# Layer norm lines in halves of 512 columns, and low weight parts formed row block by row block, in a two-layer hybrid trunk

## The chip, the cores and the metric

The kernel runs on one core of a Trainium2 chip. The time is device microseconds (us) of one execution, from launch to end; three executions of the kernel before gave a median of 1139.65 us. One more execution was recorded by the hardware profiler, and everything said about where the time goes comes from that one. TensorE (PE) multiplies matrices, VectorE (DVE) and ScalarE (ACT) work on rows of data, GpSimd (POOL) does the same more slowly, SyncE (SP) issues transfers. PEld is the loading of PE's stationary operand, which overlaps PE.

## The reference, cut to what matters

512 tokens of width 1024 go through two layers. Each has a token mixer and a dense MLP with 4096 hidden columns, and after each of these four sub-layers comes a residual sum and a layer norm.

```python
def layer_norm(x, g, b):
    xf = x.astype(jnp.float32)
    mu = jnp.mean(xf, axis=-1, keepdims=True)
    var = jnp.mean(jnp.square(xf - mu), axis=-1, keepdims=True)
    return ((xf - mu) * lax.rsqrt(var + LN_EPS) * g + b).astype(x.dtype)

def squared_relu_mlp(x, w_up, w_down):
    return jnp.square(jax.nn.relu(x @ w_up)) @ w_down

h = x
for i in range(DEPTH):                     # DEPTH = 2
    mix = dsa_mixer(h, ...) if i % 2 == 0 else gla_mixer(h, ...)
    h = layer_norm(DN_ALPHA * h + mix, ln_mix_g[i], ln_mix_b[i])
    h = layer_norm(DN_ALPHA * h + squared_relu_mlp(h, mlp_w_up[i], mlp_w_down[i]), ln_mlp_g[i], ln_mlp_b[i])
```

The first mixer is sparse attention: an indexer scores all causal keys, each query keeps the best 128 and attends to these alone. The second is gated linear attention (GLA) in chunks. All data and weights are float32.

## The kernel before, in words

**Matrix products.** Each float32 operand is split into a high part (fp32r) and a low part, the remainder. A product is three matmuls: high times high, high times low, low times high (`mm3`, lines 198, 199 and 200). Weights arrive by DMA in units of 256 rows by up to 512 columns, as a tile `raw` of two row blocks of 128 (line 133). `split` makes of such a unit `w_hi` on ACT (line 142) and `w_lo` on DVE (line 143), one operation each for both row blocks. A panel is 4 such units for most products and 7 for a step of the MLP's down product, which uses a recursive scheme with sums of weight blocks formed on POOL (`t`, lines 164 to 172). Panels are requested one ahead of use, and six buffers of each of `w_hi` and `w_lo` exist, so a unit is split when PE is done with an earlier one.

**A layer norm** takes one tile of 128 tokens by 1024 columns. Per token tile: the last matmul result is added in (`accumulate`, line 291, which also sums the row), ACT squares and sums (line 303), DVE forms the variance (lines 317 to 320, `ve` being the last), ACT takes the root (line 269), DVE refines the reciprocal (lines 270 to 273). Two long lines on DVE do the rest: line 325, `y = (y - mean) * g`, and line 326, `y = y * r + b`. Before, each is one operation of 1024 columns, except in the last layer norm, where each is two of 512, since the result goes out by halves.

**The handoff.** After a layer norm the tile is turned for the next product: `to_xt` lets PE do eight 128x128 transposes in two groups of four, one group for each half of the columns (line 247, tile `tps`); ACT copies each group to the high part of `XT` (line 250) and DVE forms the low part (line 251). PE's program goes on with other matmuls between a tile's last product and its transposes.

**Order.** Each engine runs its instructions in one fixed order, which a scheduler chooses when the program is built, from priorities (`urgent` raises them) and its own estimates of durations. An instruction waits on semaphores for others; all behind it on the same engine wait with it. So the place of the transposes among the matmuls in PE's order says when the scheduler thought the layer norm would be ready.

**Stages** by the time at which they run in the profile: sparse attention with its projections to about 222 us, its layer norm to 256, the first MLP to 560, its layer norm, overlapped with the first GLA products, to 592, GLA to 785, its layer norm to 810, the second MLP to 1115, the last layer norm and the output to the end. The GLA stage has small masked products: `prepare` builds the tiles `Q` and `E` on POOL, ACT and DVE, `apply` multiplies them on PE into `qk` (lines 1025 and 1034) and DVE takes the result over into `near` (lines 1039 and 1048).

Of the kernel before, what the change touches and what calls it, by code (L numbers as in the profile page):

```python
# [14 lines left out]
F32 = mybir.dt.float32  # L15
# [11 lines left out]
DM = 1024  # L27
# [79 lines left out]
class Trunk:  # L107
    def __init__(self, tc, es):
        self.tc, self.nc = tc, tc.nc
        self.const = es.enter_context(tc.tile_pool(name="const", bufs=1))  # L110
        self.small = es.enter_context(tc.tile_pool(name="small", bufs=4))
        self.xt_p = es.enter_context(tc.tile_pool(name="xt", bufs=1))
        self.XT = self.xt_p.tile([P, 2, KT, SEQ], F32R, name="XT")
        self.raw_p = es.enter_context(tc.tile_pool(name="raw", bufs=RAW_BUFS))
        self.w_p = es.enter_context(tc.tile_pool(name="w", bufs=W_BUFS))
        self.mm = es.enter_context(tc.tile_pool(name="mm", bufs=3, space=PSUM))
        self.qk = es.enter_context(tc.tile_pool(name="qk", bufs=2, space=PSUM))
        self.po = es.enter_context(tc.tile_pool(name="po", bufs=1, space=PSUM))
        self.tp = es.enter_context(tc.tile_pool(name="tp", bufs=2, space=PSUM))
        self.big = es.enter_context(tc.tile_pool(name="big", bufs=4))  # L120
        self.sums = [self.const.tile([P, 2], F32, name=f"sums{t}") for t in range(NT)]
        self.panels = []
        self.pending, self.turns, self.depth = [], 0, 1
        self.loaded = []
        self.taken = 0


    def fetch(self, w, r0, cols):
# [8 lines left out]
    def split(self, src):  # L137

        n = src.shape[2]
        hi = self.w_p.tile([P, 2, 512], F32R, name="w_hi")[:, :, :n]  # L140
        lo = self.w_p.tile([P, 2, 512], F32R, name="w_lo")[:, :, :n]
        self.nc.scalar.copy(hi, src)  # L142
        self.nc.vector.tensor_sub(lo, src, hi.bitcast(F32))  # L143
        return hi, lo

    def _load(self, i):
# [160 lines left out]
    def layer_norm(self, y, s, st, g, b, out=None):  # L307

        nc = self.nc
        d = self.small.tile([P, 1], F32, name="d")
        e = self.small.tile([P, 1], F32, name="e")
        nmu = self.small.tile([P, 1], F32, name="nmu")
        ve = self.small.tile([P, 1], F32, name="ve")
        nc.vector.tensor_sub(d, s[:, 0:1], s[:, 1:2])
        nc.vector.tensor_scalar(nmu, s[:, 0:1], s[:, 1:2], -1.0 / DM, op0=OP.add, op1=OP.mult)
        nc.vector.scalar_tensor_tensor(e, d, -1.0 / DM, d, op0=OP.mult, op1=OP.mult)
        nc.vector.tensor_scalar(ve, e, st["q"][:, 0:1], st["q"][:, 1:2], op0=OP.add, op1=OP.add)  # L320
        r = self.rsqrt(ve, 1.0 / DM)
        step = DM if out is None else DM // 2
        for c in range(0, DM, step):
            cs = slice(c, c + step)
            nc.vector.scalar_tensor_tensor(y[:, cs], y[:, cs], nmu, g[:, cs], op0=OP.add, op1=OP.mult)
            nc.vector.scalar_tensor_tensor(y[:, cs], y[:, cs], r, b[:, cs], op0=OP.mult, op1=OP.add)
            if out is not None:
                nc.sync.dma_start(out[:, cs], y[:, cs])
# [301 lines left out]
    def attention(self, x, xs):  # L630

        nc, tc = self.nc, self.tc
        with tc.tile_pool(name="att", bufs=1) as ap:
# [70 lines left out]
            def top_k():  # L704

                for b in range(1, NT):
                    for i in range(TOP_K // 8):
                        m8 = self.small.tile([P, 8], F32, name="m8")
                        nc.vector.max(out=m8, in_=sc[b])  # L709
                        nc.vector.match_replace(out=sc[b], in_to_replace=m8, in_values=sc[b], imm_value=NEG_TAKEN)  # L710
                        if i == TOP_K // 8 - 1:
                            nc.vector.tensor_scalar(sc[b], sc[b], NEG_SPLIT, -BIG, op0=OP.is_ge, op1=OP.mult)
                        if i % 4 == 3:
                            yield
# [107 lines left out]
            def blocks():  # L822

                for j in range(4):
                    logits(0, j)
                turned = []
                for i, (b, g) in enumerate(steps):
                    if (b, g) == (STACKED, 0):
                        split_v()
                    for x in range(4):  # L830
                        if i + 1 < len(steps):
                            logits(i + 1, x)
                        if x <= b:
                            turn(i, x)
                            if b >= STACKED:
                                turned.append((i, x))
                        if len(turned) > LAG:
                            values_t(*turned.pop(0))
                    if i > 0 and steps[i - 1][0] < STACKED:
                        values(i - 1)  # L840
                    yield
                for a in turned:
                    values_t(*a)
                for f in live.pop("back"):
                    f()

            with tc.tile_pool(name="rt", bufs=2) as self.rt, tc.tile_pool(name="p", bufs=2) as pp, \
                    tc.tile_pool(name="pT", bufs=8) as ptp, tc.tile_pool(name="on", bufs=1) as op_:
                self.rt_h = 8
                tk, bl = top_k(), blocks()  # L850
                for _ in range(4):
                    next(tk)
                u = self.next_panel()
                for t in range(NT):
                    ps = self.natural(u, t, 0, 512)
                    self.stack_q(self.rotated(ps, t, 8), 8, qT[t][:, 0:8, :])
                    next(tk)
                at = [0]

                def item():  # L860
                    next(bl)
                    if 3 <= at[0] < 7:
                        next(tk)
                    at[0] += 1

                u = self.next_panel()
                for t in range(NT):
                    ps = self.natural(u, t, 0, 512)
                    self.stack_q(self.rotated(ps, t, 8), 8, qT[t][:, 8:16, :])
                    if t % 2:  # L870
                        for _ in range(A_KV):
                            item()
                self.flush()
                wu = self.next_panel()
                for _ in range(A_KV):
                    item()
                self.load_residual(x)
                for t in range(NT - 1):
                    item()
                    self.out_first(wu, t)  # L880
                for _ in bl:
                    pass
                self.out_first(wu, NT - 1)
# [394 lines left out]
```

## Time and profile before

| what | value |
|---|---|
| median of three executions | 1139.65 us (1139.53 to 1140.13) |
| the profiled execution's own time | 1141.91 us |
| its span, first to last instruction | 1140.1 us |
| mean granted clock of TensorE | 0.991 |
| DVE busy | 888.6 us in 1592 instructions |
| ACT busy | 564.0 us |
| POOL busy | 213.7 us |

The span is 1.8 us shorter than the same execution's time, and that execution took 2.26 us longer than the median. Matmuls overlap their neighbours, so a PE that is busy need not be at its peak: the distance from one matmul's start to the next tells its pace. Idle time of an engine counts only where another one ends up waiting for it. In rows of the timeline the first two numbers are start and duration in us; a row marked x2 merges two instructions; what stands in brackets is the idle time ahead of it on its engine and what ended it.

### The profile page before, as it was taken

How to read it: one execution, taken by the hardware profiler on the slowest of the kernel's cores; microseconds unless marked ns; L12 is line 12 of the kernel's file. 1: busy time of each engine (PE TensorE's matmuls, PEld its weight loads, DVE VectorE, ACT ScalarE, POOL GpSimd, SP SyncE). 2: the span in 40 equal slices, each digit the busy share in tenths (PEclk: the TensorE clock that was granted, in tenths of full speed). 3: DMA queues.
4: the chain of work that ended last, by engine and by line, in shares of the span. 5: the costliest groups of instructions: out<-in, count | busy, mean ns of one | idle time of the engine just before them, and what ended most of it. 6: DMA issues, size and time to landing. Idle time of an engine off the chain costs nothing.

```text
span 1140.1 us, 16063 instructions
## 1 busy us (share of the span) xinstructions
PE 1124.3 (99%) x6040; PEld 948.2 (83%) x6040; DVE 888.6 (78%) x1592; ACT 564.0 (49%) x974; POOL 213.7 (19%) x136
## 2 busy tenths in 40 slices
PE   8999999999999999999999999999999999999997
PEld 7888988889888888888897897888988888888885
DVE  7899897697966976786985488667696976786787
ACT  6755686644533444444355476435353444444342
POOL 0000000002132123213300266110042123213221
PEclk9999899999999999999999999999999999999998
DMA  7222120521422422431522223152222422431421
GB/s 252 99 74 75 37 90 23 154 76 51 145 63 87 148 87 62 148 113 51 146 76 86 87 78 107 40 148 74 81 87 93 148 82 67 148 112 51 134 74 74
DMA packets 58198, 109.12 MB, mean 96 GB/s; under 512 B 5205, under 2 KB 10841, under 8 KB 58121
## 3 DMA queue, kind: packets, MB, share of 16 engines
q1 hardware_dynamic: 56968, 103.91, 29.0%
q0 software_dynamic: 1152, 4.19, 1.3%
q8 instruction: 47, 0.77, 0.3%
q14 instruction: 31, 0.25, 0.1%
HBM read 105.99 MB, written 2.10 MB: 95 GB/s over the span
## 4 chain that ended last, share of the span: by engine, by line
PE 87%; DVE 10%; issue 2%; ACT 1%; POOL 0%; DVEq 0%; ACTq 0%
PE ps L198 22%; PE ps L199 21%; PE ps L200 21%; DVE w_lo L143 2%; PE tps L247 2%; PE po L198 2%; PE po L199 2%; PE po L200 2%; PE tps L745 2%; DVE sc L710 1%; DVE m L709 1%; PE qk L200 1%; PE tps L198 1%; PE qk L198 1%; PE tps L200 1%
## 5 line engine op out<-in xcount | busy, mean ns | idle before, releaser
L143 DVE TENSOR_TENSOR w_lo<-raw,w_hi 128x1024 fp32r<-128x1024 f32 (+4 forms) x220 | 290.9, 1341 | 28.2 <-ACT w_hi L142 25.8
L142 ACT CAST w_hi<-raw 128x1024 fp32r<-128x1024 f32 (+4 forms) x220 | 223.1, 1024 | 115.6 <-PE ps L200 41.0
L198 PE MATMUL ps<-XT,w_hi 128*128 128x512 f32 (+2 forms) x648 | 237.3, 367 | 0.0
L199 PE MATMUL ps<-XT,w_hi 128*128 128x512 f32 (+2 forms) x648 | 237.2, 366 | 0.0
L200 PE MATMUL ps<-XT,w_lo 128*128 128x512 f32 (+2 forms) x648 | 237.0, 366 | 0.0
L198 PE MATMUL ps<-w_hi,XT 128*128 128x512 f32 (+4 forms) x432 | 161.9, 375 | 1.3 <-ACT w_hi L142 1.3
L199 PE MATMUL ps<-w_lo,XT 128*128 128x512 f32 (+4 forms) x432 | 158.6, 367 | 0.5 <-DVE w_lo L143 0.5
L200 PE MATMUL ps<-w_hi,XT 128*128 128x512 f32 (+4 forms) x432 | 158.6, 368 | 0.0
L198 PEld LDWEIGHTS ps<-XT,w_hi 128*128 128x128 f32 (+1 forms) x648 | 121.7, 188 | 20.3 <-issue 0.2
L199 PEld LDWEIGHTS ps<-XT,w_hi 128*128 128x128 f32 (+1 forms) x648 | 121.7, 188 | 20.2 <-issue 0.4
L200 PEld LDWEIGHTS ps<-XT,w_lo 128*128 128x128 f32 (+1 forms) x648 | 121.7, 188 | 20.2 <-issue 0.2
L164 POOL TENSOR_TENSOR raw<-raw 128x1024 f32<-128x1024 f32 x14 | 34.1, 2438 | 386.3 <-DVE w_lo L143 386.3
L200 PE MATMUL ps<-w_hi,form 128*128 128x512 f32 x260 | 101.3, 389 | 0.0
L199 PE MATMUL ps<-w_lo,form 128*128 128x512 f32 x260 | 101.3, 389 | 0.0
L198 PE MATMUL ps<-w_hi,form 128*128 128x512 f32 x260 | 101.2, 389 | 0.0
L198 PEld LDWEIGHTS ps<-w_hi,XT 128*128 128x128 f32 x432 | 81.5, 189 | 12.5 <-ACT w_hi L142 1.5
L199 PEld LDWEIGHTS ps<-w_lo,XT 128*128 128x128 f32 x432 | 81.6, 189 | 11.0 <-DVE w_lo L143 0.7
L200 PEld LDWEIGHTS ps<-w_hi,XT 128*128 128x128 f32 x432 | 81.4, 188 | 10.9
L143 DVE TENSOR_TENSOR w_lo<-t,w_hi 128x1024 fp32r<-128x1024 f32 x14 | 30.4, 2169 | 72.7 <-ACT w_hi L142 72.7
L382 DVE TENSOR_TENSOR h<-h 128x512 f32<-128x512 f32 (+1 forms) x72 | 43.9, 624 | 43.1 <-ACT h L381 43.1
L381 ACT ACTIVATE h<-ps 128x512 f32<-128x512 f32 (+1 forms) x72 | 38.9, 546 | 59.4 <-PE ps L200 51.6
L142 ACT CAST w_hi<-t 128x1024 fp32r<-128x1024 f32 x14 | 14.7, 1049 | 105.4 <-POOL t L166 105.4
(257 smaller groups left out, 1965.9 us busy)
## 6 DMA issues: line engine op xcount, KB each, us to landing
raw<-in_mlp_w_up_dram SPq DMA_DIRECT2D x64, 512.0 KB, 4.4
raw<-in_mlp_w_down_dram SPq DMA_DIRECT2D x64, 512.0 KB, 4.6
raw<-in_b_w_in_dram SPq DMA_DIRECT2D x16, 512.0 KB, 4.6
raw<-in_a_w_in_dram SPq DMA_DIRECT2D x12, 512.0 KB, 4.7
big<-in_x_dram SPq DMA_DIRECT2D x8, 512.0 KB, 4.5
raw<-in_a_w_o_dram SPq DMA_DIRECT2D x8, 512.0 KB, 4.4
raw<-in_b_w_o_dram SPq DMA_DIRECT2D x8, 512.0 KB, 5.0
raw<-in_b_w_in_dram SPq DMA_DIRECT2D x8, 346.0 KB, 3.3
```

Source lines behind the costliest of these rows:

```text
L142: self.nc.scalar.copy(hi, src)
L143: self.nc.vector.tensor_sub(lo, src, hi.bitcast(F32))
L164: sub(t1, b12, b11)
L198: mmul(out, lhs[0], rhs[0], start=first, stop=False, skip_group_check=more)
L199: mmul(out, lhs[0], rhs[1], start=False, stop=False, skip_group_check=more)
L200: mmul(out, lhs[1], rhs[0], start=False, stop=last, skip_group_check=more)
L247: nc.tensor.transpose(tps[:, j, :], src[:, k * P:(k + 1) * P], self.ident)
L381: nc.scalar.activation(h, ps[:, :step], AF.Relu)
L382: nc.vector.tensor_mul(h, h, h)
L709: nc.vector.max(out=m8, in_=sc[b])
L710: nc.vector.match_replace(out=sc[b], in_to_replace=m8, in_values=sc[b], imm_value=NEG_TAKEN)
L745: nc.tensor.transpose(tps[:, j, :], live[i][0][:, j, kb * P:(kb + 1) * P], self.ident)
```

## The change

Two edits. In `layer_norm` the two long lines now run in two halves of 512 columns in every layer norm, not the last one alone. In `split` the low part is formed by two operations, one for each row block, from a flag on that is set behind the sparse attention's last projection; every panel requested from there is split that way, which begins with the second panel of the attention's output product. The high part stays one operation.

```diff
+        self.fine = False
...
         self.nc.scalar.copy(hi, src)
-        self.nc.vector.tensor_sub(lo, src, hi.bitcast(F32))
+        for k in range(2) if self.fine else [slice(0, 2)]:
+            self.nc.vector.tensor_sub(lo[:, k], src[:, k], hi[:, k].bitcast(F32))
         return hi, lo
...
         r = self.rsqrt(ve, 1.0 / DM)
-        step = DM if out is None else DM // 2
+        step = DM // 2
         for c in range(0, DM, step):
...
                 self.flush()
+                self.fine = True
                 wu = self.next_panel()
```

Of 234 units 210 are split in two operations now, and 12 layer norms of a tile have four long lines for two: 234 instructions more on DVE. The scheduler also places other work anew, on all engines, from the sparse attention's last third on. In the changed kernel the line numbers are 2 higher from line 144 on (198 to 200 are 200 to 202, 247 is 249, 291 is 293, 325 and 326 are 327 and 328) and 3 higher behind the sparse attention (1039 is 1042, 1048 is 1051).

The first place is PE at the first token tile of the layer norm behind the first MLP: matmuls of the last down product, and the tile's transposes (`tps<-cft,big`). Before:

```order
L198 MATMUL ps<-w_hi,form 128x512
L199 MATMUL ps<-w_lo,form 128x512
L200 MATMUL ps<-w_hi,form 128x512
L198 MATMUL ps<-w_hi,form 128x512
L199 MATMUL ps<-w_lo,form 128x512
L247 MATMUL tps<-cft,big 128x128 x8
L200 MATMUL ps<-w_hi,form 128x512
```

Now:

```order
L202 MATMUL ps<-w_hi,form 128x512
L249 MATMUL tps<-cft,big 128x128 x4
L200 MATMUL ps<-w_hi,form 128x512
L249 MATMUL tps<-cft,big 128x128 x4
L201 MATMUL ps<-w_lo,form 128x512
L202 MATMUL ps<-w_hi,form 128x512
```

The eight transposes stood in one piece, and now stand in two groups of four with one matmul between. Counted over PE's whole order, the first group stands five matmuls earlier than the eight did; for the next three token tiles of this layer norm it is 4, 5 and 13 matmuls. At the layer norms behind the two mixers the same count is 1, 2, 25 and 3 (the groups 1 or 2 matmuls apart; the first tile's eight stay in one piece).

The second place is DVE in the same layer norm, from the first tile's second long line to the second tile's long lines (`sums_87` belongs to the second tile). Before:

```order
L273 TENSOR_TENSOR rr<-rr,nt_5479 128x1
L326 SCALAR_TENSOR_TENSOR big<-big,rr,lngb 128x1024
L305 TENSOR_SCALAR q<-q 128x1
L291 SCALAR_TENSOR_TENSOR big,sums_87<-big,ps 128x512
L317 TENSOR_TENSOR d<-sums_87 128x1
L318 TENSOR_SCALAR nmu<-sums_87 128x1
L319 SCALAR_TENSOR_TENSOR e<-d 128x1
L320 TENSOR_SCALAR ve<-e,q 128x1
L325 SCALAR_TENSOR_TENSOR big<-big,nmu,lngb 128x1024
L251 TENSOR_TENSOR XT<-tps,XT 128x4x128 x2
```

Now:

```order
L328 SCALAR_TENSOR_TENSOR big<-big,rr,lngb 128x512 x2
L307 TENSOR_SCALAR q<-q 128x1
L253 TENSOR_TENSOR XT<-tps,XT 128x4x128
L293 SCALAR_TENSOR_TENSOR big,sums_87<-big,ps 128x512
L253 TENSOR_TENSOR XT<-tps,XT 128x4x128
L319 TENSOR_TENSOR d<-sums_87 128x1
L320 TENSOR_SCALAR nmu<-sums_87 128x1
L321 SCALAR_TENSOR_TENSOR e<-d 128x1
L327 SCALAR_TENSOR_TENSOR big<-big,nmu,lngb 128x512
L322 TENSOR_SCALAR ve<-e,q 128x1
L327 SCALAR_TENSOR_TENSOR big<-big,nmu,lngb 128x512
```

The second tile's accumulation stood ahead of the first tile's two `XT` operations, and now stands behind the first of them; the variance stands between the halves of the first long line.

The third place is DVE in the GLA stage, where low parts stand ahead of the copies into `near`. Before:

```order
L143 TENSOR_TENSOR w_lo<-raw,w_hi 128x2x346 x2
L143 TENSOR_TENSOR w_lo<-raw,w_hi 128x1024
L1039 TENSOR_TENSOR near<-qk,eye 128x4x2x16
L143 TENSOR_TENSOR w_lo<-raw,w_hi 128x1024
L1048 COPY_PREDICATED near<-masks,qk 128x64
```

Now:

```order
L145 TENSOR_TENSOR w_lo<-raw,w_hi 128x346 x4
L145 TENSOR_TENSOR w_lo<-raw,w_hi 128x512
L1042 TENSOR_TENSOR near<-qk,eye 128x4x2x16
L145 TENSOR_TENSOR w_lo<-raw,w_hi 128x512
L1051 COPY_PREDICATED near<-masks,qk 128x64
L145 TENSOR_TENSOR w_lo<-raw,w_hi 128x512 x2
```

The first copy has half a unit's low part less ahead of it than before, the second a whole unit's: two halves now stand behind it.

## The prediction

> **What bounds the kernel now.** I read the page's busy shares first, then the stages one by one, then what PE waited for, then the timeline where the changed lines stand. Page and stages (columns: stretch, length, then busy time and instructions of PE, PEld, DVE, ACT, POOL, granted clock, DMA share, GB/s):
>
> ```profile
> PE 1124.3 (99%) x6040; PEld 948.2 (83%) x6040; DVE 888.6 (78%) x1592; ACT 564.0 (49%) x974; POOL 213.7 (19%) x136
> ...
> 106.00:110.00 4.00, 2.92 (x21) 2.13 (x20) 3.93 (x18) 3.73 (x7) 0.00 (x0) 1.00 0.01 2
> 110.00:124.00 14.00, 13.84 (x66) 13.12 (x65) 10.46 (x45) 8.16 (x20) 0.00 (x0) 0.51 0.00 1
> ...
> 160.00:222.00 62.00, 61.54 (x345) 50.77 (x344) 47.24 (x117) 44.31 (x102) 2.27 (x4) 1.00 0.23 65
> ...
> 300.00:400.00 100.00, 100.00 (x443) 82.77 (x442) 77.40 (x92) 42.03 (x54) 22.41 (x10) 1.00 0.35 111
> 560.00:592.00 32.00, 31.79 (x177) 28.01 (x175) 28.16 (x77) 15.37 (x36) 4.85 (x7) 1.00 0.30 87
> 660.00:690.00 30.00, 28.72 (x376) 25.59 (x375) 28.50 (x46) 21.84 (x40) 21.15 (x22) 1.00 0.43 133
> ```
>
> PE sets the time. In the MLPs (300 to 400) it never stops, and DVE has 22.6 us of 100 free. PE falls short only at the start, at the end, near 108 and, by tenths of a us, around the layer norms and in GLA. PE's own waits, all that bear on the change:
>
> ```profile
> PE qk L1034 <- DVE near L1048: 1.3, 2, 0.9
> PE tps L247 <- DVE big L326: 1.1, 2, 0.6
> PE ps L199 <- DVE w_lo L143: 0.5, 1, 0.5
> ```
>
> So there is little to win. PE waited for a low part once, 0.5 us, and for a layer norm's second line twice, 1.1 us.
>
> **The change part by part.** Prices first: whole and halved long lines, and an undisturbed whole low part beside two operations of 512 columns.
>
> ```profile
> L326 DVE SCALAR_TENSOR_TENSOR big<-big,rr,lngb 128x1024 f32<-128x1024 f32 x12 | 15.4, 1282 | 0.3
> ...
> 570.46 1.28 DVE L251 TENSOR_TENSOR XT<-tps,XT 128x512 fp32r<-128x512 f32 x2
> ...
> 585.89 1.20 DVE L143 TENSOR_TENSOR w_lo<-raw,w_hi 128x1024 fp32r<-128x1024 f32 x1
> ...
> 1133.25 0.75 DVE L325 SCALAR_TENSOR_TENSOR big<-big,nmu,lngb 128x512 f32<-128x512 f32 x1
> 1133.92 0.27 DVE L320 TENSOR_SCALAR ve<-e,q 128x1 f32<-128x1 f32 x1
> 1134.11 0.74 DVE L325 SCALAR_TENSOR_TENSOR big<-big,nmu,lngb 128x512 f32<-128x512 f32 x1
> 1134.76 0.16 DVE L270 RECIPROCAL rr<-rs 128x1 f32<-128x1 f32 x1
> ...
> 1135.65 1.42 DVE L326 SCALAR_TENSOR_TENSOR big<-big,rr,lngb 128x512 f32<-128x512 f32 x2
> ```
>
> Two operations take 1.28 where one takes 1.20: a split unit costs DVE 0.08 us more, 210 of them 17 us. A halved line takes 1.42 where a whole one takes 1.28, but its first half is done after 0.75. The variance can slip between the halves (0.19 from its start to the next operation), and the next operation starts 0.66 behind a half's start.
>
> **(a) Low parts in the MLPs: 0.** The down steps split 98 units, the up panels 64, the last ones 8: 170 of 210 units, 13.6 us over some 600 us. DVE's 22.6 free us in 100 hide it; with that cover gone it would cost its 13.6 us. The end is untouched, since the last layer norm was halved before.
>
> **(b) The layer norm behind the first MLP: +1.4 us.** Here PE runs on matmuls of the last down product, one every 0.23 us (443 in 100 above), then GLA products of 348 columns, one every 0.16, and each tile's transposes wait for line 326.
>
> ```profile
> 566.92 0.39 PE L199 MATMUL ps<-w_lo,form 128*128 128x512 f32 x1
> 567.53 1.09 PE L247 MATMUL tps<-cft,big 128*128 128x128 f32 x8 [0.21 <-DVE q L305]
> ...
> 574.18 0.39 PE L198 MATMUL ps<-w_hi,form 128*128 128x512 f32 x1
> 574.45 1.06 PE L247 MATMUL tps<-cft,big 128*128 128x128 f32 x8
> ...
> 589.81 0.32 PE L198 MATMUL ps<-w_hi,XT 128*128 128x348 f32 x1
> 589.97 0.32 PE L199 MATMUL ps<-w_lo,XT 128*128 128x348 f32 x1
> 590.13 1.06 PE L247 MATMUL tps<-cft,big 128*128 128x128 f32 x8
> ```
>
> Before: the slot behind 566.92 is 567.15, the transposes start at 567.53: 0.38 lost. At 574.45, 0.04 lost; at 590.13 none. DVE meanwhile:
>
> ```profile
> 563.19 0.15 DVE L319 SCALAR_TENSOR_TENSOR e<-d 128x1 f32<-128x1 f32 x1
> ...
> 564.83 0.16 DVE L270 RECIPROCAL rr<-rs 128x1 f32<-128x1 f32 x1
> ...
> 566.19 1.28 DVE L326 SCALAR_TENSOR_TENSOR big<-big,rr,lngb 128x1024 f32<-128x1024 f32 x1
> ...
> 567.45 0.68 DVE L291 SCALAR_TENSOR_TENSOR big<-big,ps 128x512 f32<-128x512 f32 x1
> ...
> 569.08 0.27 DVE L320 TENSOR_SCALAR ve<-e,q 128x1 f32<-128x1 f32 x1 [0.56 <-ACT junk L303]
> ...
> 573.01 1.29 DVE L326 SCALAR_TENSOR_TENSOR big<-big,rr,lngb 128x1024 f32<-128x1024 f32 x1
> ```
>
> First tile: `e` at 563.19, half line 563.38, `ve` 564.05, half 564.24, reciprocal 564.90 (before 564.83). The small steps and one accumulation follow as before, 1.36 us to line 326 and 0.1 more for their new order: first half at 566.35, done 567.10, PE at 567.17. That is 0.36 earlier than 567.53. But the order sends PE there five matmuls earlier, 1.13 us: it arrives at 566.02 and waits 1.15, where it waited 0.38. PE is 0.77 behind.
>
> Second tile: its accumulation started at 567.45; now its last matmul stands behind the first tile's transposes, and one `XT` operation (0.60) stands ahead of it, so it starts about 569.05, 1.6 late. The chain wins most of it back: the half line fills the 0.56 wait for ACT, and the `XT` pair's 1.20 between the lines is gone. I add the steps up to a first half done at 574.4, where the whole line ended at 574.30. PE arrives at 574.18 (26 matmuls behind 568.28) and starts at 574.5: waits 0.3, 0.04 before. Third tile: done 582.75, PE there about 582.78: 0.1 with the usual latency, 0 before. Fourth tile: two 348 halves, two 512 halves (0.61 each) and both `XT` operations stand in its chain; done 589.4, PE, 13 matmuls early, there at 589.08: waits 0.4, 0 before. Sum: 0.77 + 0.26 + 0.1 + 0.4 = 1.5, and 0.1 off for rounding my starts late: 1.4. Nothing behind gives it back, since PE is the bound up to GLA's middle. Bounds: all waits there gone, -0.4; twice the sum, +2.8.
>
> **(c) The two layer norms behind the mixers: 0.** The same steps by the same prices:
>
> ```profile
> 249.05 1.07 PE L247 MATMUL tps<-cft,big 128*128 128x128 f32 x8
> ...
> 253.91 0.28 PE L199 MATMUL ps<-XT,w_hi 128*128 128x256 f32 x1
> 254.03 0.28 PE L200 MATMUL ps<-XT,w_lo 128*128 128x256 f32 x1
> 254.85 1.07 PE L247 MATMUL tps<-cft,big 128*128 128x128 f32 x8 [0.55 <-DVE big L326]
> ```
>
> Before, PE lost 0.25, 0.17 (at 249.05) and 0.71 (at 254.85) behind the second, third and fourth tile: 1.1. Now the third tile's first half is ready 2.7 us sooner than its whole line was (246.2 for 248.9), since three whole low parts in its chain became four halves and the next accumulation moved behind it; but PE comes 25 matmuls of 256 columns sooner, 0.12 each, 3.0 us. I get waits of 0.24, 0.45 and 0.43: 1.1 again. Bounds for each of the two: -1.1 and +1.1.
>
> **(d) GLA: -0.1.** The two waits of PE for `near` lie here, 0.39 and 0.89 us in the rows, both behind low parts that POOL's work slows.
>
> ```profile
> 660.64 3.76 DVE L143 TENSOR_TENSOR w_lo<-raw,w_hi 128x692 fp32r<-128x692 f32 x3 [0.24 <-ACT w_hi L142]
> ...
> 681.06 4.75 DVE L143 TENSOR_TENSOR w_lo<-raw,w_hi 128x1024 fp32r<-128x1024 f32 x3
> 685.87 1.52 DVE L143 TENSOR_TENSOR w_lo<-raw,w_hi 128x1024 fp32r<-128x1024 f32 x1
> 687.31 0.22 DVE L1048 COPY_PREDICATED near<-masks,qk 128x64 f32<-128x64 uint8 x1
> 687.44 0.97 DVE L1008 TENSOR_TENSOR E<-E,gk 128x512 f32<-128x512 f32 x1
> ```
>
> The first goes, as two halves move behind the copy (-0.5 with its latency). The second does not: the `E` at 687.44 feeds the same matmuls and still comes after all four units, now with four times 0.08 and one copy (0.13 from 687.31 to 687.44) more ahead: +0.4. Bounds: both gone, -1.3; the four units dearer by half of a contended one's 1.5, +0.8.
> [...] The rows above show 0.08 for low parts and 0.14 for a long line. [...]
>
> **(e) The sparse attention's last third: 0.** Its order is dealt anew from about 160 to 222. PE idles there for 62.00 - 61.54 = 0.46 us, so no more is to be gained. What the new order loses no row shows; the nearest is the stretch 106 to 110, where PE led the same logits and idled 1.08 of 4 us. I take 0 with bounds -0.5 and +2.2 (twice that).
>
> Sum: 0 + 1.4 + 0 - 0.1 + 0 = **+1.3**: 1141.91 to 1143.2 for the profiled execution's own time, and as it lay 2.26 above the median, 1139.65 to **1141.0**.
>
> **The rivals.** *The handoffs win* (0.10). The scheduler moved the transposes up because it expects the layer norms sooner; if DVE keeps that date, the waits go: 0.4 in (b), 1.1 twice in (c), 0.5 in (d) and 0.4 in (e): -3.5, 1136.2. For it: an undisturbed halved layer norm has its first half ready some 0.7 us sooner (0.53 by the half, the rest by the filled wait for ACT). Against: PE was moved up by as much or more.
> *DVE is later still* (0.17). In (b) each tile's accumulation waits behind `XT` operations that wait for transposes that wait for the layer norm, so one late tile makes the next late. The price is (b) twice, +2.8, and half of (c)'s upper bound in each, +1.1: with (d) +3.8, 1143.5. It decides as soon as the first wait exceeds about 1.5 us. For it: DVE is busy 28.16 of 32.00 us there. Against: I found the second tile recovering.
> *The clock falls* (0.04). The stretch 110 to 124 runs at 0.51 right behind the idle of 106 to 110. If a wait of 1.15 us does that at 567, dense matmuls take twice as long: over 14 us that is up to 7 us, 1148. Against: PE waited 0.89 at 687 with the granted clock at 1.00 throughout 660 to 690.
> [...]
> *The halves do nothing* (0.14): PE hardly waits for low parts, and the handoffs come out even: 1139.6.
>
> **How the numbers follow.** The forecast has 0.55. A difference under 0.2%, 2.3 us, cannot be told from none: below 1137.4 is faster, above 1141.9 slower. Forecast and "nothing" lie inside, but the forecast's upper side, with (e)'s loss, crosses 1141.9 with about 0.06. Slower: 0.17 less a fifth that ends inside, plus 0.04 and 0.06, 0.24; faster 0.09; same 0.67. The range: (b) to its half and (e) to its gain below, most of the "later still" case above: 1138.3 to 1143.3.
>
> **What would show it.** Right: at the layer norm behind the first MLP PE's first transposes wait about 1.1 us, the fourth tile's some 0.4; the `near` wait near 665 is gone, that near 688 stays; PE without a gap in the MLPs; DVE busy some 17 to 20 us more. Wrong: transposes without waits (the handoffs win), a first wait over 1.5 us, a second stretch at half clock, or new PE idle between 160 and 222, which would put the sum where I have nothing.

## The result: the changed kernel is slower

| | before | changed |
|---|---|---|
| median, 16 executions each | 1141.10 us | 1146.22 us |
| lowest and highest | 1139.53, 1144.81 | 1144.67, 1150.87 |
| span of the profiled execution | 1140.1 us | 1144.2 us |
| DVE busy | 888.6 us | 908.4 us |

The ratio of the times is 1.0052 with a 95% interval of 1.0039 to 1.0065, so about 5.9 us are lost of 1140 (the medians of the table alone differ by 5.1). The forecast was 1141.0 with a range of 1138.3 to 1143.3; the time lies outside, on the slow side.

What PE waited for in the changed kernel, and the stretches at which the prediction looked (the columns are those of its own fences: stretch, length, busy time and instructions of PE, PEld, DVE, ACT and POOL, granted clock, DMA share, GB/s):

```profile
PE tps L249 <- DVE big L328: 3.5, 1, 3.5
PE qk L1037 <- DVE E L1011: 1.6, 1, 1.6
PE qk L1037 <- DVE near L1051: 0.6, 1, 0.6
```

```profile
PE 1125.4 (98%) x6040; PEld 946.9 (83%) x6040; DVE 908.4 (79%) x1826; ACT 566.2 (49%) x974; POOL 213.7 (19%) x136
...
160.00:222.00 62.00, 61.95 (x341) 50.38 (x340) 47.76 (x121) 43.75 (x101) 2.28 (x4) 1.00 0.28 83
300.00:400.00 100.00, 100.00 (x443) 82.84 (x442) 77.70 (x117) 40.41 (x52) 24.68 (x11) 1.00 0.36 111
560.00:592.00 32.00, 28.45 (x156) 24.26 (x155) 30.13 (x89) 15.82 (x36) 2.41 (x5) 1.00 0.28 80
660.00:690.00 30.00, 29.21 (x351) 26.22 (x349) 28.25 (x52) 23.17 (x45) 17.43 (x22) 1.00 0.33 100
688.00:692.00 4.00, 2.44 (x47) 1.80 (x46) 4.00 (x9) 1.60 (x4) 1.76 (x2) 1.00 0.77 212
692.00:696.00 4.00, 4.00 (x11) 3.14 (x12) 2.78 (x7) 1.64 (x5) 3.68 (x4) 0.57 0.57 202
```

One wait stands out: 3.5 us for the first tile behind the first MLP, at 564 to 568. In 560 to 592 PE works 28.45 of 32 us, where it worked 31.79. A second wait has grown at 690, and the 4 us behind it run at a mean clock of 0.57. The inside of the MLP and the sparse attention's last third lose nothing.

The whole distance can be placed by three instants that both kernels have: the first transposes behind the first mixer, behind the first MLP and behind the second mixer. Before (the middle one, 567.53, stands in the prediction) and last matmul:

```profile
231.70 0.27 PE L247 MATMUL tps<-cft,big 128*128 128x128 f32 x1
...
785.96 0.28 PE L247 MATMUL tps<-cft,big 128*128 128x128 f32 x1
...
1131.58 0.39 PE L200 MATMUL ps<-w_hi,form 128*128 128x512 f32 x1
```

The changed kernel:

```profile
229.60 0.38 PE L249 MATMUL tps<-cft,big 128*128 128x128 f32 x2
...
567.84 0.66 PE L249 MATMUL tps<-cft,big 128*128 128x128 f32 x4 [3.48 <-DVE big L328]
...
790.19 0.38 PE L249 MATMUL tps<-cft,big 128*128 128x128 f32 x2
...
1135.87 0.39 PE L202 MATMUL ps<-w_hi,form 128*128 128x512 f32 x1
```

From the first instant to the second it took 335.83 before and 338.24 now, in which four matmuls less stand (0.9 us): +3.3 for the same work. From the second to the third 218.43 and 222.35, with four matmuls more: +3.0. From the third to the end 345.62 and 345.68 with one more: -0.2. Sum +6.1, close to the 5.9 of the ratio. What lies ahead of the first instant differs from execution to execution by the stretches at half clock near the start and near 110 (before: none near the start, 13.65 us from 110.24 on; the changed kernel: 3.41 us near 10 and 3.41 near 112) and is left out.

**Why the first transposes wait.** DVE ahead of this layer norm, before:

```profile
556.70 0.87 DVE L143 TENSOR_TENSOR w_lo<-raw,w_hi 128x696 fp32r<-128x696 f32 x1
557.50 0.68 DVE L475 SCALAR_TENSOR_TENSOR big<-big,tps 128x512 f32<-128x512 f32 x1
558.09 1.38 DVE L143 TENSOR_TENSOR w_lo<-raw,w_hi 128x696 fp32r<-128x696 f32 x1
559.40 0.68 DVE L291 SCALAR_TENSOR_TENSOR big<-big,ps 128x512 f32<-128x512 f32 x1
```

Now, and POOL beside it:

```profile
556.24 0.51 DVE L145 TENSOR_TENSOR w_lo<-raw,w_hi 128x348 fp32r<-128x348 f32 x1
556.67 0.68 DVE L477 SCALAR_TENSOR_TENSOR big<-big,tps 128x512 f32<-128x512 f32 x1
557.27 4.07 DVE L145 TENSOR_TENSOR w_lo<-raw,w_hi 128x348 fp32r<-128x348 f32 x3
561.27 0.68 DVE L293 SCALAR_TENSOR_TENSOR big<-big,ps 128x512 f32<-128x512 f32 x1
...
564.16 0.75 DVE L327 SCALAR_TENSOR_TENSOR big<-big,nmu,lngb 128x512 f32<-128x512 f32 x1
...
567.03 1.42 DVE L328 SCALAR_TENSOR_TENSOR big<-big,rr,lngb 128x512 f32<-128x512 f32 x2
```

```profile
556.24 4.72 POOL L480 TENSOR_TENSOR big<-big 128x512 f32<-128x512 f32 x3
```

Two low parts of 696 columns took 0.87 and 1.38 us. As four pieces of 348 columns the first takes 0.51, and the three that follow 4.07 together, while POOL does its three last additions of the MLP. Four pieces cost 4.6 us where two cost 2.25, and the layer norm's accumulation follows without a gap, 2.3 us later by that alone. All behind it, down to the first half of L328, is late by as much.

### The profile page after: what moved, and what is told of

Same layout as the page of the kernel before. It is cut to its first block, busy times and chain, and to the rows that moved or that the text cites. A ratio compares the mean times of both kernels' runs of the same rounds, so it can differ in the third digit from the quotient of the medians.

```text
span 1144.2 us, 16410 instructions
## 1 busy us (share of the span) xinstructions
PE 1125.4 (98%) x6040; PEld 946.9 (83%) x6040; DVE 908.4 (79%) x1826; ACT 566.2 (49%) x974; POOL 213.7 (19%) x136
## 4 chain that ended last, share of the span: by engine, by line
PE 87%; DVE 9%; issue 2%; ACT 2%; POOL 0%; DVEq 0%; ACTq 0%
PE ps L200 22%; PE ps L202 22%; PE ps L201 22%; DVE w_lo L145 3%; PE tps L249 2%; PE po L202 2%; PE po L200 2%; PE po L201 2%; DVE sc L712 1%; DVE m L711 1%; PE tps L747 1%; PE tps L202 1%; PE qk L202 1%; PE tps L200 1%; PE qk L200 1%
## 5 line engine op out<-in xcount | busy, mean ns | idle before, releaser
L145 DVE TENSOR_TENSOR w_lo<-raw,w_hi 128x512 fp32r<-128x512 f32 (+5 forms) x416 | 315.9, 794 | 26.4 <-ACT w_hi L143 25.1
L145 DVE TENSOR_TENSOR w_lo<-t,w_hi 128x512 fp32r<-128x512 f32 x28 | 31.3, 1156 | 73.4 <-ACT w_hi L143 73.4
L174 POOL TENSOR_TENSOR raw<-t,raw 128x1024 f32<-128x1024 f32 x14 | 38.9, 2781 | 118.1 <-ACT w_hi L143 118.1
```

Of the source, the lines that this page charges most:

```text
L145: self.nc.vector.tensor_sub(lo[:, k], src[:, k], hi[:, k].bitcast(F32))
L174: sub(t4, t2, b21)
```

## The experiments

Two theories went into the first runs. **Turns** (A in the texts below): a low part on DVE and an addition on POOL do not run together; each waits until the other's running one has ended, so two pieces wait twice. **Handoff** (B): the halved lines and the earlier transposes make the wait, and the low parts are innocent. (In the two runs on the price itself, the rival B is sharing: the two engines slow each other by one factor.)

**The halved lines alone.** All low parts whole again:

```diff
                 self.flush()
-                self.fine = True
                 wu = self.next_panel()
```

> The layer norm lines in halves, every low part in one operation as before. Theory A (turns): a low part and an addition on POOL cannot run at the same time, each waits until the other's running one has ended; so the split low parts beside the sums on POOL at the end of the first MLP made DVE 2.5 us late, and that made the first transposes behind the first MLP wait 3.65 us for 1.15. By A the first transposes wait here about 1.15 us, the wait near 689 stays at 1.06 as before the change, and the time is 1.0 to 1.5 us above the kernel before. Theory B (handoff): the halved lines and the transposes moved up five matmuls make the wait, and the low parts are innocent. By B the first transposes wait 3 us or more here too, and the time is 3 to 6 us above the kernel before.

Measured: ratio to the kernel before 0.9984 (0.9966 to 1.0001), and in a second set of executions, below, 0.9976 (0.9958 to 0.9993). The first transposes behind the first MLP:

```profile
564.27 0.66 PE L249 MATMUL tps<-cft,big 128*128 128x128 f32 x4 [0.81 <-DVE big L328]
```

A wait is measured from here on as the distance from the start of the matmul ahead to the start of the transposes, less the usual 0.23 from one matmul to the next. So PE loses 0.97 us here; it is 3.65 in the changed kernel, and was 1.15 in the prediction. The handoff theory falls: the halves and the earlier order are all here, and the wait is a quarter. The wait near 689 is 1.06, as the theory of turns has it. The expected time was wrong: not 1 us above the kernel before, but some 2 below by the ratios, 0.9 below by the three instants.

**The low parts alone.**

```diff
-        step = DM // 2
+        step = DM if out is None else DM // 2
```

> The low parts in two operations, the layer norm lines whole as before; the transposes behind the first MLP stand where they stood before. A (turns): the same DVE delay of 2.5 us without the earlier transposes: the first transposes wait 0.38 + 2.5 = 2.9 us, the wait near 689 is 1.5 to 1.9, and the time is 3.5 to 5.5 us above the kernel before. B (handoff): the first transposes wait 0.4 to 0.6, and the time is within 1 us of the kernel before.

Measured: 1.0064 (1.0042 to 1.0085), some 7 us slower. The intervals do not tell it from the whole change, which it reaches without the halved lines; the theory of turns had expected 3.5 to 5.5. The wait is 3.4 us, where 2.9 was expected, though the transposes stand where they stood:

```profile
568.74 1.65 PE L249 MATMUL tps<-cft,big 128*128 128x128 f32 x7 [3.26 <-DVE q L307]
```

**Only the units of 348 columns whole again.**

```diff
-        for k in range(2) if self.fine else [slice(0, 2)]:
+        for k in range(2) if self.fine and n != 348 else [slice(0, 2)]:
```

> The changed kernel, but the low parts of the units of 348 columns (those that DVE forms beside the sums on POOL ahead of the layer norm behind the first MLP) in one operation. Nothing else stands otherwise ahead of the first transposes. A (turns): they wait 1.15 us for 3.65, so the time is 2.5 us below the changed kernel, about 3.5 us above the kernel before; the rest is lost in GLA. B (handoff): they wait 3.3 to 3.7 us as in the changed kernel, and the time is that of the changed kernel.

Measured: 1.0023 (1.0008 to 1.0038), 3.3 us less than the change by the two ratios, and the wait is 1.7 us for 3.65:

```profile
560.24 0.87 DVE L145 TENSOR_TENSOR w_lo<-raw,w_hi 128x696 fp32r<-128x696 f32 x1
...
561.63 1.38 DVE L145 TENSOR_TENSOR w_lo<-raw,w_hi 128x696 fp32r<-128x696 f32 x1
562.93 0.68 DVE L293 SCALAR_TENSOR_TENSOR big<-big,ps 128x512 f32<-128x512 f32 x1
```

The two durations of before are back, and 2.0 us of the wait are gone. The wait is not 1.15. What is left goes, as far as the rows show, to the halves of 512 columns ahead, which still meet POOL's additions (1.41 and 1.18 us in this run, at 556 to 559, where the price alone is 0.69).

**The price measured apart.** A kernel with nothing but streams: low parts on DVE alone, then beside additions on POOL of two SBUF tiles, each stream in a section of its own.

```python
section(lambda: V.tensor_sub(lo, raw, hi), 4)                                # L144
section(lambda: V.tensor_sub(lo[:, :512], raw[:, :512], hi[:, :512]), 6)     # L145
section(lambda: V.tensor_sub(lo[:, :256], raw[:, :256], hi[:, :256]), 8)     # L146
...
section(lambda: V.tensor_sub(lo, raw, hi), 6,                                # L148
        lambda: G.tensor_add(po[:, :512], p1[:, :512], p2[:, :512]), 9)      # L149
...
section(lambda: V.tensor_sub(lo[:, :512], raw[:, :512], ps), 6,              # L160, ps in PSUM
        lambda: G.tensor_add(po[:, :512], p1[:, :512], p2[:, :512]), 9)
```

> Only the prices: the trunk is left out; streams of low parts on DVE (1024, 512 and 256 columns) alone and beside a stream of additions on POOL (512 columns, once 256, once 1024), then other operations of DVE and copies of ACT beside it. A (turns): DVE's distance from one start to the next is its own time plus one addition on POOL, whatever the columns: beside additions of 512 columns (about 1.2 us) 2.4 us for 1024 columns, 1.8 for 512, 1.5 for 256, so that 1024 columns cost 2.4, 3.6 or 6 us; operations of 512 columns take about 1.25 beside additions of 256 and 3.0 beside additions of 1024. B (both merely slow each other down by sharing): one factor for all sizes, some 1.5 to 2 times the time alone, the sum over 1024 columns the same within 20% in one, two or four operations.

Each row gives the shortest, the median and the longest duration in ns. The shortest is that of the first operations, before POOL has begun; the median is the state in which both streams run. L144 to L147 run alone. Beside additions of 512 columns: L148 to L152 and L158 to L164; L154 is beside additions of 256 columns, L156 beside 1024.

```profile
L144 DVE TENSOR_TENSOR lo<-raw,hi x4: 1224/1226/1226, 6.5 to 10.3; 128x1024 fp32r<-128x1024 f32 x4
L145 DVE TENSOR_TENSOR lo<-raw,hi x6: 691/692/693, 11.8 to 15.4; 128x512 fp32r<-128x512 f32 x6
L146 DVE TENSOR_TENSOR lo<-raw,hi x8: 424/426/426, 16.3 to 19.6; 128x256 fp32r<-128x256 f32 x8
L147 POOL TENSOR_TENSOR po<-p,p x6: 1261/1262/1262, 20.5 to 27.2; 128x512 f32<-128x512 f32 x6
L148 DVE TENSOR_TENSOR lo<-raw,hi x6: 1224/2166/2166, 28.7 to 37.9; 128x1024 fp32r<-128x1024 f32 x6
L149 POOL TENSOR_TENSOR po<-p,p x9: 1259/2122/2242, 30.1 to 45.2; 128x512 f32<-128x512 f32 x9
L150 DVE TENSOR_TENSOR lo<-raw,hi x8: 691/1632/1635, 46.7 to 56.5; 128x512 fp32r<-128x512 f32 x8
L152 DVE TENSOR_TENSOR lo<-raw,hi x10: 424/1366/1369, 64.9 to 75.6; 128x256 fp32r<-128x256 f32 x10
L154 DVE TENSOR_TENSOR lo<-raw,hi x8: 691/1095/1097, 83.7 to 90.8; 128x512 fp32r<-128x512 f32 x8
L156 DVE TENSOR_TENSOR lo<-raw,hi x6: 691/2710/2711, 98.3 to 108.0; 128x512 fp32r<-128x512 f32 x6
L158 DVE SCALAR_TENSOR_TENSOR lo<-raw,col,hi x6: 790/1631/1632, 120.4 to 127.8; 128x512 fp32r<-128x512 f32 x6
L160 DVE TENSOR_TENSOR lo<-raw,ps x6: 686/687/689, 134.8 to 138.5; 128x512 fp32r<-128x512 f32 x6
L162 DVE TENSOR_SCALAR lo<-raw,col x6: 525/1365/1367, 147.4 to 153.6; 128x512 fp32r<-128x512 f32 x6
L164 ACT COPY act<-raw x6: 617/618/618, 161.2 to 164.4; 128x512 f32<-128x512 f32 x6
```

Beside additions of 512 columns a low part on DVE costs 0.94 us more whatever its size: 1.23 becomes 2.17, 0.69 becomes 1.63, 0.43 becomes 1.37. So 1024 columns cost 2.2 us in one operation, 3.3 in two, 5.5 in four. Beside shorter additions it is 0.40 more, beside longer ones 2.02. POOL pays as well: its addition takes 2.12 for 1.26 beside the long low parts. That is turn by turn, one operation of each, and a turn costs 0.32 us less than the addition alone (0.94 for 1.26); sharing at one common factor is out. With its second operand in PSUM the same subtraction costs 0.69 as if alone, and so do copies on ACT (0.62). The same law fits the kernel: three pieces of 348 columns (0.51 alone) at 0.94 more each are 4.35, measured 4.07.

**Shorter additions in the kernel itself.** The changed kernel, each of POOL's additions at the MLP's end in two of 256 columns:

```diff
-                    add(xn[j][:, R], xn[j][:, R], u2[:, j])
+                    for h in range(2):
+                        hs = slice(h * 256, h * 256 + 256)
+                        add(xn[j][:, R][:, hs], xn[j][:, R][:, hs], u2[:, j, hs])
...
-                        add(xn[2 + j][:, c], xn[2 + j][:, c], u3[:, j])
+                        for h in range(2):
+                            hs = slice(h * 256, h * 256 + 256)
+                            add(xn[2 + j][:, c][:, hs], xn[2 + j][:, c][:, hs], u3[:, j, hs])
```

> The changed kernel, but the additions on POOL at the end of each MLP in two operations of 256 columns for each one of 512; no instruction of DVE or PE stands elsewhere around them. Theory A: a low part beside them costs its own time plus one addition less some overlap, so shorter additions make each wait shorter. By the prices measured apart (0.94 us more beside additions of 512 columns, 0.41 beside 256) the three pieces that took 4.07 us take about 2.6 to 2.9, the first transposes wait 2.2 to 2.6 us for 3.65, and the time is about 1.2 us below the changed kernel. Theory B (sharing): the same bytes move, the three pieces still take 4 us or more, the wait stays at 3.5 or grows.

Measured: 1.0026 (1.0008 to 1.0043), about 3 us less than the change by the two ratios, whose intervals just overlap. The same three pieces, then the wait:

```profile
555.82 2.45 DVE L145 TENSOR_TENSOR w_lo<-raw,w_hi 128x348 fp32r<-128x348 f32 x3
```

```profile
565.27 0.66 PE L249 MATMUL tps<-cft,big 128*128 128x128 f32 x4 [1.75 <-DVE big L328]
```

4.07 us became 2.45 and the wait 1.9 by the measure above, though DVE does the same and POOL twice as many operations. Turns again. The gain is larger than the 1.2 us expected: the halves of 512 columns ahead are shorter as well (0.85 and 0.68 for 1.40 and 1.18), and the stretch of half clock behind 690 is not there, so the second stretch takes 220.74 us for 222.35.

**The low parts of the GLA mixer whole again**, those of the MLPs and of the first output product split:

```diff
         panel = self.panels[i]
+        self.fine = i >= 6 and not 23 <= i < 33
...
-                self.fine = True
```

> The changed kernel with the low parts of every unit of the GLA mixer (its two units rows of 348 columns, and all behind them up to its output product) in one operation again; the units of the MLPs and of the first output product stay split, the layer norm lines stay halved. Theory A (turns): the split costs only where DVE's low parts and POOL's work meet ahead of something that PE waits for, which is behind the first MLP and in GLA. So nothing is left of the loss: the first transposes behind the first MLP wait 1.0 to 1.7 us, the wait near 689 is 1.1, and the time is that of the halved layer norm lines alone, 0 to 2 us below the kernel before. Theory C (the splits in the MLPs cost too, through DVE's extra time or the sums on POOL there): the time stays 2 us or more above the halved lines alone, with new waits of PE inside the MLPs.

Measured: 1.0010 (0.9991 to 1.0028), 3 to 4 us above the halved lines alone by the ratios, 1.9 by the three instants. The two waits are as the theory of turns has them (1.7 behind the first MLP, 1.06 near 689); the time is that of the other theory, C. But C's waits inside the MLPs are not there; PE has no gap:

```profile
300.00:400.00 100.00, 100.00 (x442) 82.66 (x441) 82.29 (x124) 43.16 (x55) 20.13 (x9) 1.00 0.38 121
400.00:500.00 100.00, 100.00 (x443) 82.79 (x442) 74.42 (x105) 42.78 (x54) 29.55 (x12) 1.00 0.26 85
```

But the split of the MLPs' units costs at their edges. By the three instants, with the same places of the transposes in PE's order as in the halved lines alone: 335.92 us for 334.63 to the first MLP's layer norm (0.7 of it the wait there, 1.7 for 0.97), 219.55 for 219.54 through GLA, 345.69 for 345.05 to the end. Placed matmul by matmul, the 1.3 of the first stretch are 0.1 at the third tile behind the first mixer, 0.4 at the fourth, 0.1 where the MLP begins, nothing in the MLP, and 0.7 at the wait; behind the second mixer it is 0.2, 0.4 and 0.1. POOL does not work behind the mixers (0.00 us busy in 240 to 272 and in 800 to 820 of this run), so it is not turns there. At the fourth tile three half low parts (0.68 us each, 253.64 to 255.65) stand between its small steps and its second long line, where the halved lines alone have none, and PE waits 0.2 us for ACT's `h`; the share of each is open.

**Halved lines behind the two mixers only**, everything else as before:

```diff
-    def layer_norm(self, y, s, st, g, b, out=None):
+    def layer_norm(self, y, s, st, g, b, out=None, step=DM // 2):
...
-        step = DM // 2
...
-                        self.layer_norm(y, s, st, gb[:, 0, :], gb[:, 1, :], None if out is None else out[tok, :])
+                        self.layer_norm(y, s, st, gb[:, 0, :], gb[:, 1, :], None if out is None else out[tok, :], DM if out is None else DM // 2)
...
-                self.fine = True
```

> The kernel before with halved lines in the layer norms behind the two mixers alone; the layer norm behind the first MLP and all low parts as before. If the halves pay behind the mixers (PE's waits of 1.1 us behind each before, about 0.2 with the halves alone) and cost 0.6 us behind the MLP, this is the best of all: 1.5 to 2.5 us below the kernel before, 0.3 to 1 below the halved lines everywhere. If the halves are worth nothing anywhere, it is within 0.5 us of the kernel before.

> The halved layer norm lines alone once more, beside the others on the same chip: 0 to 2 us below the kernel before, as the first time (ratio 0.9966 to 1.0001); the first transposes behind the first MLP wait 0.97 us, as the first time.

Measured: 0.9972 (0.9954 to 0.9990) for the mixers only, 0.9976 (0.9958 to 0.9993) for the halves everywhere. Both beat the kernel before; against each other they cannot be told apart. By the three instants the mixers-only kernel needs 335.17, 218.23 and 345.05 us; with its one matmul counted in, it gains 0.9 and 0.8 behind the mixers, 1.7 of the 3.2 that the ratio says. The rest is within the interval.

**The clock.** The stretch at 0.57 behind 692 was sought in three more profiled executions of the changed kernel.

> The changed kernel once more, one execution, for the granted clock alone. If the wait of 1.7 us near 690 brings PE to half clock whenever it comes, the stretch of half clock behind it (692 to 696 the first time) is there again; if it is chance or needs something from earlier in the execution, it is missing in some of these looks, while the waits of 3.65 and 1.7 us themselves are there in each.

> A second look at the changed kernel, for the same two readings: the stretch of half clock behind 690, and the waits of 3.65 and 1.7 us.

> A third look at the changed kernel, for the same two readings: the stretch of half clock behind 690, and the waits of 3.65 and 1.7 us.

The waits of 3.65 and 1.7 us are there each time, to 0.03. Behind 692 the clock stays at 1.00 all three times. A half clock is there each time too, but elsewhere, right behind the long wait (PE busy is the first number behind the length, the clock the 1.00 or less). First and third of the three:

```profile
564.00:568.00 4.00, 0.79 (x6) 0.71 (x7) 3.81 (x13) 1.14 (x5) 0.00 (x0) 1.00 0.00 1
568.00:572.00 4.00, 4.00 (x14) 3.20 (x14) 3.23 (x10) 1.94 (x5) 0.00 (x0) 0.57 0.00 0
```

```profile
564.00:568.00 4.00, 0.53 (x3) 0.14 (x2) 3.93 (x15) 1.69 (x5) 0.00 (x0) 0.86 0.11 43
568.00:572.00 4.00, 4.00 (x14) 3.43 (x15) 2.00 (x6) 1.17 (x2) 0.00 (x0) 0.50 0.00 0
572.00:576.00 4.00, 4.00 (x15) 3.19 (x15) 3.18 (x11) 1.02 (x3) 0.00 (x0) 0.79 0.00 0
```

What it costs shows in the second stretch, from these transposes to those behind the second mixer: 222.12, 222.14 and 223.30 us in the three, 220.78 in the kernel with whole units of 348 columns, which has nearly the same order there and no half clock: 1.3, 1.4 and 2.5 us. The kernel with the low parts alone has it too behind its wait of 3.4 (clock 0.61 in 568 to 572). Where the wait was 1.7 to 1.9, in the two kernels with whole units of 348 columns and with shorter additions, the clock was 1.00 from 560 to 580. In the first profile of the changed kernel it stayed at 1.00 behind the wait of 3.65 and fell behind that of 1.7 at 690. The traces show one thing about it. A half clock that ends inside the span lasts 3.41 us in these profiles (692.28 to 695.69 in the first), or a whole number of 3.41 (13.65 near 110 in the kernel before), and within a profile the clock changes only whole numbers of 3.41 us apart (170 of them from 112.02 to 692.28 in the first). In the first profile the end of such a step, counted on from 112.02, is 566.00 and lies in the middle of the wait, so that PE was busy 1.78 us of the step ahead of it and 1.56 of the next. In the three others most of the wait lies in one step, with PE busy 1.25, 1.13 and 0.95 of its 3.41 us, and the clock falls at its end. But the step ahead of the fall at 692.28 has PE busy 1.85 us, more than the 1.56 that did nothing, so busy time alone is not the rule, and the rest is open.

## Why the prediction was wrong

**The sum, step by step.** The kernels above form a ladder, and the three instants give what each rung adds, in us:

| from one kernel to the next | predicted | measured |
|---|---|---|
| long lines in halves | most of +1.4 | -0.3, +0.2, -0.8: -0.9 |
| low parts of the MLPs and the first output product | 0 | +1.3, 0, +0.6: +1.9 |
| low parts of GLA's units but those of 348 columns | -0.1, with the next row | 0, +1.2, 0: +1.2 |
| low parts of the units of 348 columns | nothing | +2.3, +1.6 (half clock), 0: +3.9 |
| sum | +1.3 | +6.1 |

(The three numbers are those of the three stretches. In the first row they are corrected for the matmuls that moved; in the others none had to be at the instants used. The 1.6 is the second stretch of the first profile, 222.35 for 220.78, and all of it arises between 691 and 698, at the half clock; the three later profiles gave 1.3, 1.4 and 2.5. Of the +2.3, 2.0 are the wait and 0.3 a gap in PE just ahead of it, at 562.01, behind the late accumulation of 561.27.)

**The step that failed is the start of (b).** The prediction takes the first tile's `e` at 563.19 from the rows of before and works on from there. It never asked what the split does to DVE ahead of them: two units of 348 columns lie in that order, their rows (0.87 and 1.38 for the same size) already showed one disturbed, and POOL's additions stood beside it. The price "two operations take 1.28 where one takes 1.20" was read where POOL is idle, its 1.28 even from operations with one operand in PSUM (line 251), which POOL does not slow (0.69 us at L160 above, beside additions), and it was used everywhere. Only (d) had a word on "low parts that POOL's work slows", and allowed half an operation more. So the first wait was 3.65 for 1.15. For the first tile the working from `e` on was right: with all low parts whole, the same order of PE gave 0.97. For the tiles behind it was too dear: they lost 0.1, 0 and 0 us there, and 0.1, 0 and 0.1 in the changed kernel, where 0.3, 0.1 and 0.4 were worked out. So the halved lines and the new order cost 0.6 us behind the first MLP, where (b) had 1.4: the first stretch is 334.63 us with the halves everywhere, in which five matmuls less stand (1.1 us), and 335.17 with the halves behind the mixers only.

**(a)** The MLPs themselves are hidden, as said, and DVE's 19.8 us more lie in the range given; but part of that is waiting for POOL, which counts as busy (0.69 us of busy time become 1.63 at L150 above), and the units at the MLPs' edges cost 1.9 us. "The end is untouched" was right for the layer norm at the end, not for that behind the second mixer. **(c)** had 0, inside bounds of 1.1 either way: halves alone gain 0.8 to 0.9 behind each mixer, and the split takes 0.6 of it back. That this comes out near 0 is in part luck, since the prediction had waits of 1.1 us there and PE's transposes wait 0.3 and 0.5 in the changed kernel. **(d)** came out at +1.2, where -0.1 stood (third row of the table). The wait near 665 went, as said (-0.4), but one of 0.76 came near 672 (+0.8), and the wait near 688 grew from 1.06 to 1.7 (+0.6), with eight pieces ahead of `E` that take turns with POOL (the first four took 4.20 us, where four alone take 2.8):

```profile
682.94 4.20 DVE L145 TENSOR_TENSOR w_lo<-raw,w_hi 128x512 fp32r<-128x512 f32 x4
...
688.95 1.28 DVE L145 TENSOR_TENSOR w_lo<-raw,w_hi 128x512 fp32r<-128x512 f32 x2
690.15 1.10 DVE L1011 TENSOR_TENSOR E<-E,gk 128x512 f32<-128x512 f32 x1
```

From the first low part to `E` it is 7.2 us here and was 6.4 (681.06 to 687.44): 0.8 more, of which the prediction had 0.4. **(e)** was right that nothing is lost: PE idles 0.05 us in 160 to 222, where it idled 0.46.

**The rivals.** "DVE is later still" names the sign and the point (a first wait over 1.5 us), but not the mechanism: the tiles behind did not inherit it. "The clock falls" had 0.04, and it was there in every profile of the changed kernel, at 1.3 to 2.5 us for the 7 allowed. Its argument, that a wait of 0.89 does nothing, held; the waits were longer. (The idle that it names, 106 to 110, was 1.08 us; the next, 0.16, came at 111.6, when the clock had fallen.) The length of the wait alone does not tell: behind the waits of 3.4 and 3.65 us the clock fell in four profiles of five, behind that of 1.7 at 690 in one of the changed kernel's four.

## What to carry to other kernels

Before an operation on VectorE is split, look at what GpSimd does beside it: with two operands in SBUF each piece took 0.94 us more beside GpSimd additions of 1.26 us, whatever its size, so 1024 columns cost 2.2 us in one piece and 5.5 in four of 256, and the busy time hides it. Take a price from rows of the stretch where it will be paid, and work a chain on from the first operation that the change touches, not from the first row that looks like the chain's beginning. A wait on TensorE can be paid once more in clock: behind that of 3.65 us a half clock followed in three profiles of four, at 1.3 to 2.5 us.

## What was not expected of the hardware

A subtraction with one operand in PSUM runs undisturbed beside GpSimd (0.69 us for 512 columns), the same with both in SBUF takes 1.63; even a `tensor_scalar` with one long operand in SBUF and a column of scalars takes turns (1.37 for 0.53). Halving GpSimd's own operations, which makes them dearer in sum (alone 0.72 us for each of 256 columns, 1.26 for one of 512), made the changed kernel about 3 us faster: DVE's pieces wait for shorter ones (0.40 us more each beside 256 columns, 0.94 beside 512), and some 1.6 us of that is half clock that did not come.
